# Four split weight tiles, three ahead, and attention's values in an 8 KB room

## The chip, the cores and the metric

The kernel runs on one core of a Trainium2 chip. The metric is the device time of one execution in microseconds (us), lower is better. The core has five engines with a queue each: TensorE (matmul, in the profile PE, its weight loads PEld), VectorE (DVE), ScalarE (ACT), GpSimd (POOL) and SyncE (SP, which here only issues DMAs). They work side by side and wait for one another through semaphores.

## What is computed

A decoder trunk of two layers on x of 512 x 1024 in float32. The reference, cut to what matters:

```python
for l in range(DEPTH):                                   # 2
    x = x + 0.5 * swiglu(rms_norm(x, ffn1_norm[l]), ffn1_wg[l], ffn1_wu[l], ffn1_wd[l])
    h = rms_norm(x, mix_norm[l])
    z = h @ w_in[l]                                      # q | k | v | conv_B | conv_C | conv_h
    attn_out = sliding_window_attention(q, k, v, attn_sink[l])   # window 128, 8 heads of 64, 2 kv heads
    conv_out = short_conv(conv_B, conv_C, conv_h, conv_w[l])     # 3 taps
    x = x + jnp.concatenate([attn_out, conv_out], axis=-1) @ w_out[l]
    x = x + 0.5 * swiglu(rms_norm(x, ffn2_norm[l]), ffn2_wg[l], ffn2_wu[l], ffn2_wd[l])
return rms_norm(x, final_norm)
# swiglu(h, wg, wu, wd) = (silu(h @ wg) * (h @ wu)) @ wd ; d_ff = 2816
```

## The kernel before

**Split operands.** Every product of float32 operands is made of three faster matmuls. A weight tile (`raw`, 4 KB in each of the 128 partitions) is split into a high part `wh`, a cast on ScalarE (line 205), and a low part `wl`, the rest, a subtraction on VectorE (line 206, `split`). The activations are split in the same way. TensorE then adds high x high, high x low and low x high in one bank of PSUM.

**The supply of weights.** `plan` (line 420) writes down ahead of time which raw tiles are loaded (`units`) and in which order tiles are split (`order`). `need_raw` (line 191) issues the loads from SyncE's queue (line 189); a few raw tiles are sums of two weight blocks, and the second block is added by a DMA that GpSimd issues (line 200). There are eight rooms for raw tiles (`stock`, tag "raw"). `need_split` (line 215) splits all tiles up to a given place in the order, loading four units further than the one that it splits. `take_split` (line 280) hands the next split tile to a product and first asks for the splits of the tiles up to `SPLIT_AHEAD` = 2 further. Three rooms each hold `wh` and `wl`, so the split of the tile two ahead waits until TensorE is done with the tile before the present one. A product of one tile is mostly 12 matmuls.

**Order of the work.** The queues are filled from the order in which the program states the work, which is its priority; a compile-time scheduler may put a later instruction first where an earlier one isn't ready. In regions between `by_hand` and `by_itself` TensorE keeps the written order. On the chip each engine takes its queue in the order so fixed.

**The stages.** A feed-forward part is a list of stages (`FIRST`, `INNER`, `LAST`): "p" plain blocks (with `halves`, line 312, three tiles held at once and both halves of the tokens run through them, and then the `up` tile, line 1009), "w" blocks of gate and up in Winograd's form with seven products (`winograd2`, line 1080), "d" the down projection (`down`, `down_end`), "s" the down projection of four blocks in Winograd's form (`share`, line 895, seven chains of two products each; `stream`, line 878). Where `share` gets `after`, it is a *closing group*: it ends a part and feeds the next part's norm. Its chains are `CHAINS_EARLY`; after the fifth chain the norm of the first half of the tokens starts (`Norm.stage`: squares, root, the scaled `xn` of line 624), and in the seventh `pull` transposes them on TensorE (line 648) and splits them (lines 657 and 658, named `hh`, `hl` or `fb`). VectorE adds each chain's banks to the residual stream `x` (line 923; line 1240 for "d"). Three parts are closed so, the first feed-forward part of layer 0 and attention's output projection in both layers; the other parts end with `down_end`.

**Rooms for small tiles.** The tag "g2" has 14 rooms of 2 KB: gates, kept sums, the planes that a Winograd block sends through a transposing DMA (line 1103), the norms' `xn` and gains, attention's turned probabilities. The tag "g8" has four rooms of 8 KB. Attention's values `vv` (line 1407) take a raw tile's room, as do its probabilities. The bias table of attention is made once (`make_bias`, line 863) after the second "d" of the first part: an iota on GpSimd (line 865), then VectorE (line 867 on).

The functions that the diff touches:

Of the kernel before, what the change touches and what calls it, by code (L numbers as in the profile page):

```python
# [9 lines left out]
F32R = mybir.dt.float32r  # L10
# [6 lines left out]
P = 128  # L17
# [3 lines left out]
HD = 64  # L21
NH = 8
NKV = 2
FF = 2816
KC = D // P
NT = S // P
# [21 lines left out]
XT_TAGS = ("sc", "aux", "aux", "mm", "sc", "sc", "aux", "aux")  # L48

OPEN = 3  # L50
SPLIT_AHEAD = 2
LOAD_AHEAD = 4

CHAINS = (
# [19 lines left out]
def trunk_kernel(  # L74
# [28 lines left out]
    wpool = ctx.enter_context(tc.tile_pool(name="wpool", bufs=1))  # L103
# [4 lines left out]
        return ps.tile(shape, F32, tag=tag, bufs={"mm": 4, "sc": 2, "aux": 2}[tag], name=name)  # L108

    def g2(name, dt=F32, shape=(P, S)):  # L110
        return work.tile(list(shape), dt, tag="g2", bufs=14, name=name)

    def g8(name, dt=F32R, shape=(P, 2, 2, S)):
        return work.tile(list(shape), dt, tag="g8", bufs=4, name=name)
# [6 lines left out]
    def stock(name, dt=F32, shape=(P, KC, P)):  # L121
        return wpool.tile(list(shape), dt, tag="raw", bufs=8, name=name)
# [92 lines left out]
    def need_split(g):  # L215
        while state["split"] <= min(g, len(order) - 1):
            n = state["split"]
            u, what = order[n]
            far = what == "far"
            if what in (None, "wide", "room", "far"):  # L220
                need_raw(u if far else u + LOAD_AHEAD)
                raw = raw_of.pop(u)
            elif isinstance(what, tuple):

                what, h, how = what
                far = how == "far"
                last = {"a11": 0, "a12": 4, "s2": 2, "s3": 6, "s1": 2, "a22": 8, "s4": 4}[what]
                need_raw(u + h if far else u + max(last, 4) + h + LOAD_AHEAD)
                a11, s1, a12, s3, a22 = (raw_of.get(u + 2 * i + h) for i in range(5))
                if what == "s2":  # L230
                    late = state["late"] if h else None
                    with tc.issue_after(late) if late else nullcontext():
                        nc.vector.tensor_add(a11, a11, s1)  # L233
                raw = {"a11": a11, "a12": a12, "s2": a11, "s3": s3, "s1": s1, "a22": a22, "s4": a12}[what]
            else:

                need_raw(u + 4 + LOAD_AHEAD)
                a11, a12, s1, s3, a22 = (raw_of.get(u + i) for i in range(5))
                if what == "s2":
                    nc.vector.tensor_add(a11, a11, s1)  # L240
                if what == "s4":
                    nc.vector.tensor_add(a11, a11, a12)
                raw = {"a11": a11, "a12": a12, "s2": a11, "s3": s3, "s1": s1, "a22": a22, "s4": a11}[what]
                if what == FORMS[-1]:
                    for i in range(5):
                        del raw_of[u + i]
            shape = list(raw.shape)
            if what == "room":
                hi, lo = both(f"wx_{n}", shape=(P, 2, 2, S))
            else:  # L250
                hi = wpool.tile(shape, F32R, tag="wh", bufs=3, name=f"wh_{n}")
                lo = wpool.tile(shape, F32R, tag="wl", bufs=3, name=f"wl_{n}")
            if far:
                sent = split_far(hi, lo, raw)
            else:
                state["cast"] = split(hi, lo, raw)
            if isinstance(order[n][1], tuple):
                early = how == "early"
                if what == "s2" if early else what == "s3":
                    if how:  # L260
                        nc.gpsimd.dma_start(out=a12, in_=a11, accum_op=ALU.add)
                    else:
                        nc.vector.tensor_add(a12, a12, a11)
                done = {
                    "s2": (0,) if early else (),
                    "s3": (3,) if early else (0, 3),
                    "s1": (1,),
                    "a22": (4,),
                    "s4": (2,),
                }.get(what, ())  # L270
                for i in done:
                    del raw_of[u + 2 * i + h]
            split_of[n] = (hi, lo)
            state["split"] += 1
            if far:

                with tc.issue_after(sent.ins):
                    need_raw(u + LOAD_AHEAD + (4 + h if isinstance(order[n][1], tuple) else 0))

    def take_split(ahead=SPLIT_AHEAD):  # L280
        n = state["group"]
        state["group"] += 1
        need_split(n + ahead)
        return n, *split_of.pop(n)
# [27 lines left out]
    def halves(norm, n, done):  # L312

        first = state["group"]
        held = [take_split(SPLIT_AHEAD - j)[1:] for j in range(n)]
        accs = [psum("mm", [P, S], f"acc_{first + j}") for j in range(n)]
        for t in range(2):
            for half in range(2):
                for j, (hi, lo) in enumerate(held):
                    for k in range(KC // 2 * half, KC // 2 * (half + 1)):  # L320
                        xh, xl = norm.half(k, t)
                        for i, (w, x_) in enumerate(((hi, xh), (hi, xl), (lo, xh))):
                            nc.tensor.matmul(  # L323
                                accs[j][:, t * H : (t + 1) * H],
                                w[:, k, :],
                                x_,
                                start=t + k + i == 0,
                                stop=k == KC - 1 and i == 2,
                                skip_group_check=True,
                            )  # L330
                    if not t and half and j < 2:
                        norm.pull()
                    if t and half:
                        need_split(first + j + 3)
                        done(j, accs[j])

    def down(acts, blocks, open_):
# [30 lines left out]
    def down_end(acts, blocks, norm, open_):  # L368

        a, b = blocks  # L370
        held = []

        def tile_of(n):
            while len(held) <= n:
                held.append(take_split(max(0, min(SPLIT_AHEAD, 3 - len(held))))[1:])
            return held[n]

        def products(acc, t, n):
# [28 lines left out]
        for o in range(2):  # L407
            accs = {t: bank(t, o) for t in (2, 3)}
            for i in range(2):
                n = 2 * o + i  # L410
                for t in (2, 3):
                    products(accs[t], t, n)
                    if i:
                        yield t, o, accs[t]
                if n in (1, 2):
                    norm.pull()
                if n:
                    need_split(ahead + n - 1)

    def plan():  # L420
        def plain(wg, wu, b):
# [335 lines left out]
    def squares(n):  # L757
# [4 lines left out]
            )  # L762

    first = [
        tuple(wpool.tile([P, KC, P], F32R, tag=f"w{p}", bufs=3, name=f"w{p}_{n}") for p in "hl")
        for n in range(OPEN)
    ]
    opening, begun = [], set()
# [126 lines left out]
    def share(  # L895
# [6 lines left out]
        for step, (acc, operand, start) in enumerate(chains):  # L902
# [7 lines left out]
                tag = {"x": "mm", "y": "sc", "w": "aux", "z": "mm"}[acc]  # L910
                accs[acc] = [psum(tag, [P, S], f"{acc}_{ops.name}_{m}") for m in range(2)]
            for h in range(2):
                _, wh, wl = take_split()
                stream(accs[acc], wh, wl, xh, xl, h, start, after if step == 6 else None)
                each()
                if soon:
                    ops.make(*soon.get((step, h), ()))
                if h == 0 or step in kept:
                    continue
                for o, t, sign in shares[step]:  # L920
                    for m in range(2):
                        part = xt(2 * t + m, o)
                        nc.vector.scalar_tensor_tensor(  # L923
                            part, accs[acc][m], by * sign, part, op0=ALU.mult, op1=ALU.add
                        )
                        if after and (step, (o, t)) in ENDS_EARLY:
                            after(2 * t + m, o)
# [14 lines left out]
    def ffn(norm, stages, whole, after=None, late=None):  # L942
# [137 lines left out]
        def winograd2(b, at, between=None):  # L1080
# [1 line left out]

            name = f"{whole}_{b}"
            accs = {}
            gates = [g2(f"gate_{name}_{t}") for t in range(NT)]
            ups = [None] * NT
            kept = {}
            planes = []
# [23 lines left out]
            for step, (acc, operand, start) in enumerate(CHAINS):  # L1112
# [5 lines left out]
                for h in range(2):  # L1118
                    _, wh, wl = take_split()
                    stream(accs[acc], wh, wl, xh, xl, h, start)  # L1120
                    for u in range(2):
# [3 lines left out]
                        if step == 0:  # L1125
                            keep("p1", u, out)
                        if step == 1:
                            nc.vector.tensor_add(gates[u], out, kept["p1", u])
                            nc.scalar.activation(gates[u], gates[u], AF.Silu)
                        if step == 2:  # L1130
# [6 lines left out]
                        if step == 5:  # L1137
# [2 lines left out]
                            nc.vector.tensor_mul(ups[u], ups[u], gates[u])  # L1140
                            apart(u)
                        if step == 6:
                            nc.scalar.activation(gates[2 + u], out, AF.Silu)
                            nc.vector.tensor_mul(ups[2 + u], ups[2 + u], gates[2 + u])
                            apart(2 + u)
# [230 lines left out]
    def mix(l, norm, after):  # L1376
# [20 lines left out]
        def take_values():  # L1397
# [6 lines left out]
                )  # L1404


            vv = stock(f"vv_{l}", F32R, (P, NT * NKV, 2, HD))
            vsrc = vp.rearrange("p t g d -> p (t g) d")
            nc.scalar.copy(vv[:, :, 0, :], vsrc)
            nc.vector.tensor_sub(vv[:, :, 1, :], vsrc, f32(vv[:, :, 0, :]))  # L1410
# [197 lines left out]
```

## Time and profile before

| what | value |
| --- | --- |
| median of 3 runs | 1654.36 us (1653.59 to 1654.96) |
| the profiled execution, whole | 1655.61 us |
| its span, first to last instruction | 1653.8 us |
| granted clock of TensorE, mean | 0.999 |
| DMA, mean over the span | 184 GB/s |

The profile is of one execution. Its page gives each engine's busy time and share of the span, the chain of work that ended last and the costliest groups; the trace behind it answers for waits (who stood idle until whom), for timelines of an engine, and for tiles. An instruction is named by its line in the kernel, its engine and `out<-in`, by the program's tile names without their numbers.

### The profile page before, as it was taken

The numbers are of one execution on the slowest core, as the hardware profiler recorded it, in microseconds if no ns is written. First come the engines' busy times: TensorE is split into PE (matmuls) and PEld (weight loads), VectorE is DVE, ScalarE is ACT, GpSimd is POOL, SyncE is SP. The second block draws the span as 40 slices with busy tenths as digits, with TensorE's granted clock in tenths as the row PEclk, the third lists the DMA queues.
The fourth block names the chain that finished last, engine by engine and source line by source line (L and its number), as shares of the span: only waits on it lengthen the run. The fifth ranks groups of instructions, "written<-read, shape, count | busy, mean of one in ns | idle before, by whom it ended". The sixth has DMA issues, their size and how long they took to land.

```text
span 1653.8 us, 21619 instructions
## 1 busy us (share of the span) xinstructions
PE 1639.9 (99%) x7912; PEld 1377.6 (83%) x7912; DVE 1307.0 (79%) x1712; ACT 1092.4 (66%) x1527; POOL 192.7 (12%) x172
## 2 busy tenths in 40 slices
PE   9999999999999999999999999999999999999998
PEld 7878888888889888888898888888988888888886
DVE  7977779867799777789797777896587987777895
ACT  6457787556566567776565777864565765777864
POOL 0011111100111101111001111110001101111111
PEclk9999999999999999999999999999999999999999
DMA  9378999821495779999837789996125946899992
GB/s 255 91 189 204 226 214 267 209 78 52 110 241 121 194 187 222 211 227 250 223 85 197 197 211 221 237 248 184 52 65 143 225 115 167 218 225 219 235 261 76
DMA packets 273791, 303.97 MB, mean 184 GB/s; under 512 B 89332, under 2 KB 157972, under 8 KB 273684
## 3 DMA queue, kind: packets, MB, share of 16 engines
q1 hardware_dynamic: 231156, 223.27, 45.8%
q0 software_dynamic: 41824, 78.65, 28.1%
q8 instruction: 62, 1.02, 0.2%
q10 hardware_dynamic: 704, 0.66, 0.1%
q14 instruction: 45, 0.37, 0.1%
HBM read 263.74 MB, written 2.10 MB: 161 GB/s over the span
## 4 chain that ended last, share of the span: by engine, by line
PE 92%; DVE 5%; ACT 1%; issue 1%; DMA 0%; POOL 0%; DVEq 0%; ACTq 0%; POOLq 0%
PE x L884 25%; PE y L884 12%; PE x_s L884 10%; PE w L884 6%; PE y_s L884 5%; PE acc L296 4%; PE acc L297 4%; PE acc L299 4%; PE down L346 3%; PE w_s L884 3%; PE acc L323 3%; PE x_m L884 2%; DVE wl L206 2%; PE up L1009 1%; PE acc L782 1%; DVE x L923 1%
## 5 line engine op out<-in xcount | busy, mean ns | idle before, releaser
L206 DVE TENSOR_TENSOR wl<-raw,wh 128x1024 fp32r<-128x1024 f32 (+1 forms) x493 | 597.4, 1215 | 227.0 <-ACT wh L205 220.6
L205 ACT CAST wh<-raw 128x1024 fp32r<-128x1024 f32 (+1 forms) x493 | 515.1, 1046 | 391.3 <-PE y L884 61.4
L884 PE MATMUL x<-wh,fb 128*128 128x512 f32 x608 | 187.3, 389 | 0.1
L884 PE MATMUL y<-wh,ft 128*128 128x512 f32 x608 | 187.1, 389 | 0.0
L884 PE MATMUL x<-wh,ft 128*128 128x512 f32 x608 | 187.1, 389 | 0.0
L884 PEld LDWEIGHTS y<-wh,ft 128*128 128x128 f32 x608 | 114.1, 188 | 23.7
L884 PEld LDWEIGHTS x<-wh,ft 128*128 128x128 f32 x608 | 114.1, 188 | 23.7
L884 PEld LDWEIGHTS x<-wh,fb 128*128 128x128 f32 x608 | 113.9, 188 | 23.9 <-DVE x L1240 0.5
L884 PE MATMUL x<-wl,fb 128*128 128x512 f32 x304 | 118.3, 389 | 0.0
L884 PE MATMUL x<-wl,ft 128*128 128x512 f32 x304 | 118.3, 389 | 0.0
L884 PE MATMUL y<-wl,ft 128*128 128x512 f32 x304 | 118.3, 389 | 0.0
L1155 ACT COPY raw_a<-pt 128x1024 uint16<-128x1024 uint16 x76 | 103.3, 1359 | 13.0 <-DMA pt<-pl 12.9
L200 POOL DMA_DIRECT2D raw<-in_ffn_wu_dram x39 | 47.2, 1211 | 517.4 <-DMA raw<-in_ffn_wu_dram 360.8
L296 PE MATMUL acc<-hh,wh 128*128 128x512 f32 x240 | 94.6, 394 | 0.0
L299 PE MATMUL acc<-hh,wl 128*128 128x512 f32 x240 | 93.9, 391 | 0.0
L297 PE MATMUL acc<-hl,wh 128*128 128x512 f32 x240 | 93.6, 390 | 0.0
L884 PE MATMUL w<-wh,fb 128*128 128x512 f32 x304 | 93.5, 389 | 0.0
L200 POOL DMA_DIRECT2D raw<-in_ffn_wg_dram x39 | 47.4, 1222 | 275.3 <-DMA raw<-in_ffn_wu_dram 70.7
L884 PE MATMUL x_s<-wh,ft_s 128*128 128x512 f32 x256 | 78.8, 389 | 0.0
L884 PE MATMUL y_s<-wh,ft_s 128*128 128x512 f32 x256 | 78.8, 389 | 0.0
L884 PE MATMUL x_s<-wh,fb_s 128*128 128x512 f32 x240 | 73.9, 389 | 0.0
L233 DVE TENSOR_TENSOR raw<-raw,raw 128x1024 f32<-128x1024 f32 x58 | 70.8, 1221 | 2.3 <-DMA raw<-in_ffn_wd_dram 1.6
(361 smaller groups left out, 3452.3 us busy)
## 6 DMA issues: line engine op xcount, KB each, us to landing
raw<-in_ffn_wu_dram SPq DMA_DIRECT2D x126, 512.0 KB, 4.7
raw<-in_ffn_wd_dram SPq DMA_DIRECT2D x104, 512.0 KB, 6.7
raw<-in_ffn_wg_dram SPq DMA_DIRECT2D x86, 512.0 KB, 4.9
raw<-in_ffn_wu_dram POOLq DMA_DIRECT2D x39, 512.0 KB, 7.3
raw<-in_ffn_wg_dram POOLq DMA_DIRECT2D x39, 512.0 KB, 5.8
raw<-in_w_in_dram SPq DMA_DIRECT2D x36, 512.0 KB, 3.9
raw<-in_ffn_wd_dram POOLq DMA_DIRECT2D x32, 512.0 KB, 8.2
raw<-raw POOLq DMA_DIRECT2D x20, 512.0 KB, 8.2
```

The lines of the kernel that those rows point to most:

```text
L200: nc.gpsimd.dma_start(out=r, in_=rows_of(*more), accum_op=ALU.add)
L205: cast = nc.scalar.copy(hi, raw)
L206: eng.tensor_sub(lo, raw, f32(hi))
L233: nc.vector.tensor_add(a11, a11, s1)
L296: nc.tensor.matmul(acc, hi[:, k, :], rhs[k][0], start=k == first, stop=False)
L297: nc.tensor.matmul(acc, hi[:, k, :], rhs[k][1], start=False, stop=False)
L299: nc.tensor.matmul(acc, lo[:, k, :], rhs[k][0], start=False, stop=k == last)
L323: nc.tensor.matmul(accs[j][:, t * H : (t + 1) * H], w[:, k, :], x_, start=t + k + i == 0, stop=k == KC - 1 and i == 2, skip_group_check=True,)
L346: nc.tensor.matmul(acc, a[:, k, tok], w[:, k, :], start=i + k + n == 0 and fresh[t], stop=i == last and k == 1 and n == 2, skip_group_chec ...
L782: nc.tensor.matmul(opening[n], (lo if part == "w" else hi)[:, k, :], xl if part == "x" else xh, start=n not in begun, stop=k == KC - 1 and ...
L884: nc.tensor.matmul(accs[u], x_[:, 2 * h + k, tok], w[:, k, :], start=start and h + k + i == 0, stop=h + k == 2 and i == 2, skip_group_chec ...
L1155: nc.scalar.copy(room.rearrange("p c (n z) -> p c z n", z=2)[:, :, z, :], turned[0][:, NT * z + 2 * c : NT * z + 2 * c + 2, :],)
```

## The change

The split tiles get a fourth room, and the look-ahead goes from two to three, except in the first eight tiles and, in closing groups, in the steps 4 and 5 (the fifth and sixth chain), where it stays two. The places where tiles are held (`halves`, `down_end`) ask one tile further as well. To make room, the small tiles lose three of their 14 rooms, and `winograd2` makes its four gates when they are first written and not all at the start. Attention's values move from the tag "raw" to the tag "g8".

```diff
-SPLIT_AHEAD = 2
+SPLIT_AHEAD = 3
...
     def g2(name, dt=F32, shape=(P, S)):
-        return work.tile(list(shape), dt, tag="g2", bufs=14, name=name)
+        return work.tile(list(shape), dt, tag="g2", bufs=11, name=name)
...
-                hi = wpool.tile(shape, F32R, tag="wh", bufs=3, name=f"wh_{n}")
-                lo = wpool.tile(shape, F32R, tag="wl", bufs=3, name=f"wl_{n}")
+                hi = wpool.tile(shape, F32R, tag="wh", bufs=4, name=f"wh_{n}")
+                lo = wpool.tile(shape, F32R, tag="wl", bufs=4, name=f"wl_{n}")
...
     def take_split(ahead=SPLIT_AHEAD):
         n = state["group"]
+        ahead = min(ahead, 2) if n < 8 else ahead
...
                     if t and half:
-                        need_split(first + j + 3)
+                        need_split(first + j + SPLIT_AHEAD + 1)
...
-                held.append(take_split(max(0, min(SPLIT_AHEAD, 3 - len(held))))[1:])
+                held.append(take_split(min(SPLIT_AHEAD, 4 - len(held)))[1:])
...
                 if n:
-                    need_split(ahead + n - 1)
+                    need_split(ahead + n)
...
-        tuple(wpool.tile([P, KC, P], F32R, tag=f"w{p}", bufs=3, name=f"w{p}_{n}") for p in "hl")
+        tuple(wpool.tile([P, KC, P], F32R, tag=f"w{p}", bufs=4, name=f"w{p}_{n}") for p in "hl")
...
-                _, wh, wl = take_split()
+                _, wh, wl = take_split(SPLIT_AHEAD - 1 if after and step in (4, 5) else SPLIT_AHEAD)
...
-            gates = [g2(f"gate_{name}_{t}") for t in range(NT)]
+            gates = [None] * NT
...
                         if step == 1:
+                            gates[u] = g2(f"gate_{name}_{u}")
...
                         if step == 6:
+                            gates[2 + u] = g2(f"gate_{name}_{2 + u}")
...
-            vv = stock(f"vv_{l}", F32R, (P, NT * NKV, 2, HD))
+            vv = g8(f"vv_{l}", F32R, (P, NT * NKV, 2, HD))
```

## The prediction

> **What bounds the kernel now.** I read the page first, then the waits of TensorE, then the timelines of the engines around those waits.
>
> ```profile
> span 1653.8 us, 21619 instructions
> PE 1639.9 (99%) x7912; PEld 1377.6 (83%) x7912; DVE 1307.0 (79%) x1712; ACT 1092.4 (66%) x1527; POOL 192.7 (12%) x172
> ```
>
> TensorE is idle for 13.9 us of the span, the start and the end of the program included, so no deeper buffer can win more than a fraction of a per cent. The waits of TensorE (tile and line; what it waited for; us in total, times, longest) name the candidates:
>
> ```profile
> PE acc L323 <- DVE wl L206: 1.9, 3, 0.6
> PE x_m L884 <- DVE wl L206: 1.6, 2, 0.8
> PE idle L141 <- DVE warm L728: 1.2, 1, 1.2
> PE down L346 <- DVE x L1240: 0.9, 2, 0.5
> PE up L1009 <- DVE wl L206: 0.8, 3, 0.3
> PE xt L747 <- DMA x<-in_x_dram: 0.3, 1, 0.3
> ```
>
> Three of the six are for `wl`, the low part of a split weight tile, which is what a fourth tile can reach. The view counts idle time only after the modelled end of a matmul; what a wait costs is read from start to start in TensorE's timeline (start, us, then the instruction, the idle time before it in brackets):
>
> ```profile
> 479.27 0.39 PE L884 MATMUL y_m<-wl,ft_m 128*128 128x512 f32 x1
> 479.50 1.07 PE L884 MATMUL x_m<-wh,ft_m 128*128 128x512 f32 x4
> 481.34 0.50 PE L884 MATMUL x_m<-wl,ft_m 128*128 128x512 f32 x1 [0.78 <-DVE wl L206]
> 481.68 0.63 PE L884 MATMUL x_m<-wh,ft_m 128*128 128x512 f32 x2
> ...
> 504.15 0.40 PE L323 MATMUL acc<-fb,wh 128*128 128x256 f32 x2
> ...
> 505.58 0.40 PE L323 MATMUL acc<-fb,wh 128*128 128x256 f32 x2
> 506.08 0.39 PE L323 MATMUL acc<-fb,wl 128*128 128x256 f32 x1
> ...
> 507.38 0.40 PE L323 MATMUL acc<-fb,wh 128*128 128x256 f32 x2
> 508.42 0.39 PE L323 MATMUL acc<-fb,wl 128*128 128x256 f32 x1 [0.63 <-DVE wl L206]
> ...
> 511.16 1.03 PE L648 MATMUL xt<-ident,xn 128*128 128x128 f32 x8
> ...
> 524.40 0.40 PE L1009 MATMUL up<-fb,wh 128*128 128x256 f32 x2
> 525.08 0.38 PE L1009 MATMUL up<-fb,wl 128*128 128x256 f32 x1 [0.28 <-DVE wl L206]
> ```
>
> Wide matmuls start 0.23 us apart (479.27 to 479.50), so a product of 12 takes 2.7 us. In `x_m` four run ahead of the first `wl`, which was due at 479.50 + 4 x 0.23 = 480.41 and came at 481.34: 0.93 lost, and 0.11 more at the next start (0.34 instead of 0.23). Matmuls of 256 columns start 0.12 apart (two in 0.40 of which one lasts 0.28). The `wl` of `acc` was due at 505.82 and 507.62 and came 0.26 and 0.80 late, that of `up` 0.44 late; with 0.1 for each restart these are 1.26 and 0.54.
>
> The waits view gives the repeats. `x_m` occurs twice, 2 x 1.04 = 2.1 us. `up` occurs three times, 3 x 0.54 = 1.6 us. The pair in `acc` occurs three times (the view counts the longer of each pair), 3 x 1.25 = 3.7 us. Together that is 7.4 us that TensorE loses for split weights. The `down` waits are for something else, below.
>
> **The change part by part.** The fourth pair of `wh` and `wl` with three ahead moves every split one product earlier against TensorE; it adds no instruction. Each split is still one cast on ScalarE and one subtraction on VectorE, and each still waits for the room of the product just finished. What goes is the case in which an engine stood idle for a room and was then too busy:
>
> ```profile
> 463.15 1.06 ACT L205 CAST wh<-raw 128x1024 fp32r<-128x1024 f32 x1 [4.57 <-PE acc L297]
> ...
> 511.79 1.08 ACT L657 CAST fb<-xt 128x512 fp32r<-128x512 f32 x2 [3.03 <-PE xt L648]
> ...
> 521.60 1.05 ACT L205 CAST wh<-raw 128x1024 fp32r<-128x1024 f32 x1 [0.28 <-PE acc L323]
> ```
>
> ```profile
> 463.45 0.69 DVE L1556 TENSOR_TENSOR m<-acc,cc 128x512 f32<-128x512 f32 x1 [2.53 <-PE acc L299]
> ...
> 478.34 1.22 DVE L687 TENSOR_TENSOR sums_m<-sums_m,m 128x1024 f32<-128x1024 f32 x1
> ...
> 480.07 1.22 DVE L206 TENSOR_TENSOR wl<-raw,wh 128x1024 fp32r<-128x1024 f32 x1
> ...
> 498.89 2.48 DVE L923 SCALAR_TENSOR_TENSOR x<-x_m,x 128x512 f32<-128x512 f32 x4
> 501.29 1.22 DVE L206 TENSOR_TENSOR wl<-raw,wh 128x1024 fp32r<-128x1024 f32 x1
> 502.42 2.48 DVE L658 TENSOR_TENSOR fb<-xt,fb 128x512 fp32r<-128x512 f32 x4
> 504.81 1.22 DVE L206 TENSOR_TENSOR wl<-raw,wh 128x1024 fp32r<-128x1024 f32 x1
> 505.94 1.29 DVE L923 SCALAR_TENSOR_TENSOR x<-z_m,x 128x512 f32<-128x512 f32 x2
> 507.14 1.22 DVE L206 TENSOR_TENSOR wl<-raw,wh 128x1024 fp32r<-128x1024 f32 x1
> 508.27 0.16 DVE L616 TENSOR_TENSOR v<-ss 128x2 f32<-128x2 f32 x1
> ...
> 509.45 2.74 DVE L624 SCALAR_TENSOR_TENSOR xn<-x,y,gain 128x512 f32<-128x512 f32 x4
> ```
>
> (1) `x_m`, at the fourth product of attention's closing group. Ahead of that group ScalarE stands 4.57 us and VectorE 2.53; a cast and a subtraction fit in there. VectorE then works from 463.45 without a pause up to the late `wl` at 480.07, so one subtraction less (1.13 from start to start, 501.29 to 502.42) brings it forward by 1.13, and in the program it now also stands ahead of the sum at 478.34. Lost were 1.04: I take the whole 2.1 us. If VectorE's order eats it, 0.
>
> (2) `up`, the fourth tile after three that are held together. With three rooms its cast can't start before the first held tile is done (521.60). With four it can start when the three begin, and ScalarE is idle for 3.03 us before 511.79. I take the whole 1.6 us.
>
> (3) `acc`, the first tiles after a closing group. In that group's fifth and sixth product the look-ahead stays at two, so nothing is gained there; at the seventh two splits are asked for at once. VectorE has no pause between 498.89 and 508.27, so a `wl` done earlier pushes something else back. Either the splits of the fifth and sixth product are pulled forward into short pauses, the fourth room allowing it, and all 3.7 us go; or the second `wl` runs in front of the four residuals `fb` of 502.42. Then the first two of those end at 503.55 + 2 x 0.60 = 504.75 instead of 503.62, while TensorE wants them at 504.27: 0.5 late and 0.1 for the restart; the `x` of 505.94 starts 1.13 later, and so does the `xn` of 509.45, whose second of four then ends at 509.45 + 1.13 + 2 x 0.67 = 511.9. Its four transposes, 0.11 apart, end at 512.4; today the eight of 511.16 are through at 512.0. So the two late `wl` go, and TensorE is still some 0.5 later than today: 3 x 0.5 = 1.5 us worse. Between -3.7 and +1.5 I take -1.9, half of the gain: the `wl` of 507.14 belongs to a later statement than the norm's `v` of 508.27 and still runs first, so idle moments are filled, but few are left.
>
> (4) `down`:
>
> ```profile
> 110.19 1.21 POOL L200 DMA_DIRECT2D raw<-in_ffn_wg_dram  x1 [10.99 <-DMA raw<-in_ffn_wu_dram]
> ...
> 111.80 0.46 DVE L867 CAST dist<-dist_i 128x256 f32<-128x256 int32 x1 [3.47 <-POOL dist_i L865]
> ...
> 112.13 0.39 PE L346 MATMUL down<-wl,a 128*128 128x512 f32 x1
> 112.90 0.73 PE L346 MATMUL down<-wh,a 128*128 128x512 f32 x2 [0.38 <-DVE x L1240]
> ```
>
> VectorE stands 3.47 us behind the bias table's iota, and GpSimd's iota behind a DMA issue that waits for a landing; the reads `x` of the banks queue after it. This start was due at 112.36 and came 0.54 late, 0.65 with its restart; of the two waits and one shorter one behind them I make 1.8. An earlier load could win that, a later one lose as much; 0.
>
> (5) Eleven small rooms instead of fourteen, and gates made when first written. A grouped product writes fourteen of them, the last four being planes that leave by a transposing DMA, placed one to four products into the next block (this row is from the answer on the tile `pl`):
>
> ```profile
> DMA to landing us min/median/max: 3.2/4.4/8.5
> ```
>
> Room by room in turn, the sixth write of a block then takes the room of the first plane: gone by 2.7 + 8.5 = 11.2 us, asked for after six products, 16.3 us. 5 us are to spare; 0. If that fails, an evacuation of a bank comes late.
>
> (6) Attention's values in an 8 KB room: the same cast and subtraction. Four such rooms exist, and attention holds two (its mixed outputs) until the closing group's sums take one. One more raw tile may load ahead there, where no row shows TensorE waiting. 0. In the first eight tiles the look-ahead stays at two: 0.
>
> Sum: 2.1 + 1.6 + 1.9 = 5.6 us. The profiled execution took 1655.61 (its span and 1.8 around it), 1.25 above the median, so 1650.0 on its own clock and **1654.36 - 5.6 = 1648.8** on the median's.
>
> A rule of the Trainium skill speaks against part (3): "TensorE: Matmul & The Clock Gate", Architectural detail, says that VectorE and ScalarE run strictly first in, first out. By that rule nothing jumps a queue on the chip, and only the order fixed before the run counts, which no row of this trace shows for the new kernel; with it (3) is +1.5, the first rival's time.
>
> **The rivals.** *The closing groups only trade waits* (3 at its bad end): -2.1 - 1.6 + 1.5 = -2.2, 1652.2. For it: VectorE is full there. Against: the filled gap above.
>
> *All split waits go, and `down` with them*: -7.4 - 1.8 = -9.2, 1645.2. Against: (3).
>
> *Slower: the raw tiles aren't there yet.* ScalarE's waits have this row:
>
> ```profile
> ACT wh L205 <- DVE raw L233: 15.8, 7, 2.9
> ```
>
> Seven casts already stand behind a sum of two raw tiles. Asked for 2.7 us earlier, with loads that don't come earlier, each blocks ScalarE for up to 2.9 + 2.7 = 5.6 us, and VectorE's `wl` and the bank reads `x` behind it. TensorE returns to a bank after two products (5.4 us), of which two reads take 1.3, so from a block of 4.1 us on it waits: 1.5 each, 10.5 for seven, less 5.6 won: +4.9, 1659.3. Against: a load waits for a raw room that a split frees, and splits come earlier as well; today none of these seven reaches TensorE.
>
> *It doesn't do what it says*: the engines' order leaves the splits where they are; 1654.4.
>
> **How the numbers follow.** Forecast 0.47; all waits gone 0.13; trading 0.17; no effect 0.05; slower 0.18. About 0.2% (3.3 us) is what a measurement of this kernel can tell from no change. Faster is 0.47 + 0.13 = 0.60; within is 0.17 + 0.05 = 0.22; slower 0.18. The range goes from all gone (1644.9, with 0.3 of scatter) to 1656.0, a slower case of which a third of the blocks bite; most of the 0.18 stays outside.
>
> **What would show it.** Right: no row of TensorE waiting for `wl` under `x_m` and `up`; the ScalarE pause before attention's closing group holds a cast; the rows under `acc` shorter but there. Wrong: new rows of TensorE waiting for `fb`, `hl` or `xn` (trading), for `x` (slower), ScalarE's waits for `raw` sums well above 15.8, or waits on `pl`.

## The result, and the profile after

The changed kernel takes 1652.12 us (median of 13 executions, 1650.4 to 1654.99), the kernel before beside it 1655.96 (13 executions, 1653.59 to 1657.79). The ratio is 0.9977, interval 0.9968 to 0.9985: 3.8 us faster, hardly more than the 0.2% that can be told from no change. A second measurement gave 1652.93 against 1655.69, ratio 0.9983 (0.9974 to 0.9991). The forecast was 1648.8: the sign was right, the time is 3.3 us above it and inside the range.

The profiled execution of the changed kernel took 1650.43, against 1655.61 before: 5.2 less, where the sum said 5.6. From its page, span and busy time:

```profile
span 1648.7 us, 21650 instructions
PE 1637.2 (99%) x7912; PEld 1376.7 (84%) x7912; DVE 1303.5 (79%) x1712; ACT 1089.3 (66%) x1527; POOL 193.0 (12%) x172
```

And all that is left of TensorE's waits (tile, line, what it waited for; us in total, times, longest):

```profile
PE xt L649 <- DVE xn L625: 2.1, 3, 0.8
PE idle L141 <- DVE warm L729: 1.2, 1, 1.2
PE xt L748 <- DMA x<-in_x_dram: 1.0, 1, 1.0
```

No wait for `wl` is left, under `x_m`, `up` or `acc`; `down` is gone too; the norm's `xn` is new. Read from start to start in TensorE's timeline, as the prediction did, the three kinds of `wl` wait gave back their whole 2.1 + 1.6 + 3.7 us, small `wl` waits too short for the list another 0.3, and `down` 1.8. Lost again were 3.4 before the `xn` transposes (0.8, 1.3 and 1.3), 0.6 more in attention's two closing groups and 0.3 near 29 us. Net 5.2; the spans differ by 5.1. The longer wait for `x` at the start costs nothing: the transposes ahead of it begin 0.64 earlier, and the first product starts at 6.66 instead of 6.65.

**Where `xn` became late.** VectorE, then ScalarE, then TensorE of the changed kernel, at the end of the closing group of attention in layer 0:

```profile
491.74 0.15 DVE L617 TENSOR_TENSOR v<-ss 128x2 f32<-128x2 f32 x1
492.65 1.22 DVE L206 TENSOR_TENSOR wl<-raw,wh 128x1024 fp32r<-128x1024 f32 x1 [0.76 <-ACT wh L205]
...
493.94 0.68 DVE L924 SCALAR_TENSOR_TENSOR x<-x_m,x 128x512 f32<-128x512 f32 x1
...
495.87 2.73 DVE L625 SCALAR_TENSOR_TENSOR xn<-x,y,gain 128x512 f32<-128x512 f32 x4
```

```profile
491.57 1.05 ACT L205 CAST wh<-raw 128x1024 fp32r<-128x1024 f32 x1
492.52 0.29 ACT L618 ACTIVATE r<-v,eps 128x2 f32<-128x2 f32 x1
```

```profile
495.45 0.39 PE L885 MATMUL z_m<-wl,fb_m 128*128 128x512 f32 x1
496.67 1.32 PE L649 MATMUL xt<-ident,xn 128*128 128x128 f32 x8 [0.84 <-DVE xn L625]
```

VectorE of the kernel before, at the same place:

```profile
493.92 0.16 DVE L616 TENSOR_TENSOR v<-ss 128x2 f32<-128x2 f32 x1 [0.15 <-ACT sq L592]
...
495.10 2.74 DVE L624 SCALAR_TENSOR_TENSOR xn<-x,y,gain 128x512 f32<-128x512 f32 x4
```

Before, `xn` began 1.18 after `v` (493.92 to 495.10); now it takes 4.13 (491.74 to 495.87). A cast of a later weight tile stands ahead of the norm's root `r` on ScalarE, and its subtraction and three reads `x` of banks stand ahead of `xn` on VectorE. The order fixed before the run had a free room for that split and took it. TensorE starts 1.22 after its last matmul instead of 0.23.

**Why `down` is no longer late.** VectorE of the changed kernel, at the end of the first "d":

```profile
108.41 2.48 DVE L1243 SCALAR_TENSOR_TENSOR x<-down,x 128x512 f32<-128x512 f32 x4
111.08 1.23 DVE L206 TENSOR_TENSOR wl<-raw,wh 128x1024 fp32r<-128x1024 f32 x1 [0.20 <-ACT wh L205]
112.22 0.68 DVE L1243 SCALAR_TENSOR_TENSOR x<-down,x 128x512 f32<-128x512 f32 x1
112.82 0.28 DVE L868 CAST dist<-dist_i 128x256 f32<-128x256 int32 x1
```

Five of the bank reads `x` now stand ahead of `dist`, and `dist` finds the iota done. Before, only two did; VectorE stood 3.47 us behind the iota, and the other reads queued behind it. The iota itself was no earlier than before (GpSimd began it at 111.24, before at 110.93).

### The profile page after: what moved, and what is told of

The parts are those of the page before. It is cut to its first block, busy times and chain, and to the rows that moved or that the text cites. A ratio compares the mean times of both kernels' runs of the same rounds, so it can differ in the third digit from the quotient of the medians.

```text
span 1648.7 us, 21650 instructions
## 1 busy us (share of the span) xinstructions
PE 1637.2 (99%) x7912; PEld 1376.7 (84%) x7912; DVE 1303.5 (79%) x1712; ACT 1089.3 (66%) x1527; POOL 193.0 (12%) x172
## 4 chain that ended last, share of the span: by engine, by line
PE 96%; DVE 2%; ACT 1%; DMA 1%; issue 0%; SPq 0%; ACTq 0%; DVEq 0%
PE x L885 25%; PE y L885 13%; PE x_s L885 10%; PE w L885 6%; PE y_s L885 5%; PE acc L324 5%; PE acc L297 4%; PE acc L298 4%; PE acc L300 4%; PE down L347 3%; PE w_s L885 3%; PE up L1010 1%; PE xt L649 1%; PE y_m L885 1%; PE x_m L885 1%; PE acc L783 1%
```

## Experiments

My theory at this point: the fourth room does the work, and what the change lost again it lost in the order of the closing groups. Rivals: the earlier asking does the work (e2); the moves of small tiles and of attention's values do part of it (e3, e12); the losses come from DMA landings (e7, e10).

**e1: four rooms, look-ahead two as before.** From the changed kernel:

```diff
-SPLIT_AHEAD = 3
+SPLIT_AHEAD = 2
...
-        ahead = min(ahead, 2) if n < 8 else ahead
...
-                held.append(take_split(min(SPLIT_AHEAD, 4 - len(held)))[1:])
+                held.append(take_split(max(0, min(SPLIT_AHEAD, 3 - len(held))))[1:])
...
-                    need_split(ahead + n)
+                    need_split(ahead + n - 1)
...
-                _, wh, wl = take_split(SPLIT_AHEAD - 1 if after and step in (4, 5) else SPLIT_AHEAD)
+                _, wh, wl = take_split()
```

> Fourth room, eleven small rooms and the values' move as in the changed kernel, but every look-ahead as before (two). Theory 1, the room alone is enough, because the order fixed before the run fills idle moments with later splits as soon as their room is free: TensorE's waits for wl under x_m and up go, 3 to 4 us less than before (ratio 0.9975 to 0.998). Rival, the asking is what counts: all wl waits of before are still there (4.3 us in the waits view) and the time is that of before (ratio 0.9995 to 1.0005).

Measured: 1650.51 (1649.83 to 1651.94), ratio to the kernel before 0.9966 (0.9954 to 0.9979). Waits of its TensorE:

```profile
PE xt L648 <- DVE xn L624: 1.7, 2, 0.8
PE idle L141 <- DVE warm L728: 1.2, 1, 1.2
PE xt L747 <- DMA x<-in_x_dram: 0.7, 1, 0.7
```

No wait for `wl`, though no split is asked for earlier than before. The room does it, with the moves that make place for it and without the earlier asking: the compile-time order fills it by itself.

**e2: look-ahead three, three rooms.** The changed kernel with three rooms (the list of the first tiles likewise):

```diff
-                hi = wpool.tile(shape, F32R, tag="wh", bufs=4, name=f"wh_{n}")
-                lo = wpool.tile(shape, F32R, tag="wl", bufs=4, name=f"wl_{n}")
+                hi = wpool.tile(shape, F32R, tag="wh", bufs=3, name=f"wh_{n}")
+                lo = wpool.tile(shape, F32R, tag="wl", bufs=3, name=f"wl_{n}")
```

> The changed kernel with three rooms for wh and wl instead of four; the look-ahead stays three. Theory 1 (the room is what was missing): the casts wait for their room as before, the wl waits come back (4.3 us in the waits view), the time is before's or up to 3 us above (ratio 0.9995 to 1.002). Rival (asking earlier in the program is enough): the wl waits stay away and the ratio is 0.997 to 0.998.

Measured: 1658.13 (1656.63 to 1661.18), ratio 1.0012 (1.0004 to 1.0021). Its TensorE:

```profile
PE xt L649 <- DVE xn L625: 1.3, 3, 0.4
PE x_s L885 <- DVE wl L206: 1.3, 3, 0.5
...
PE acc L324 <- DVE fb L659: 1.0, 2, 0.5
PE y_m L885 <- ACT wh L205: 0.8, 2, 0.4
```

Asking earlier does take away the waits under `x_m`, both of them, and two of three under `up`. But `xn`, `x_s`, `fb` and others wait in their place: asking alone loses. Ahead of `fb`, VectorE now takes two subtractions in a row (from 501.61), and `acc` waits 0.5 for it.

**e3: the moves alone.** The kernel before with eleven small rooms, gates made when first written and the values in the 8 KB room:

```diff
-        return work.tile(list(shape), dt, tag="g2", bufs=14, name=name)
+        return work.tile(list(shape), dt, tag="g2", bufs=11, name=name)
...
-            gates = [g2(f"gate_{name}_{t}") for t in range(NT)]
+            gates = [None] * NT
...
-            vv = stock(f"vv_{l}", F32R, (P, NT * NKV, 2, HD))
+            vv = g8(f"vv_{l}", F32R, (P, NT * NKV, 2, HD))
```

> The kernel before with eleven small rooms, late gates and the values in an 8 KB room, and no change to the splits. Theory: the moves cost and win nothing, the waits of TensorE stay as before, ratio 0.9995 to 1.0005. Rival: the two waits of down at 113 and 115 us, which the changed kernel lost, went because the small rooms changed the order around the bias table; then they are gone here as well and the ratio is about 0.999.

Measured: 1655.86 (11 executions), ratio 0.9997 (0.9988 to 1.0006): nothing.

```profile
PE acc L323 <- DVE wl L206: 1.9, 3, 0.6
PE x_m L884 <- DVE wl L206: 1.6, 2, 0.8
PE w_s L884 <- DVE wl L206: 1.4, 1, 1.4
```

The waits for `wl` are all there. The `down` waits happened to be missing with VectorE's order unchanged: the iota came at 109.78 instead of 110.93, since the DMA that GpSimd waited for (10.99 us before) had landed sooner. So `down` also hangs on a landing that differs between executions.

**e4: three ahead in the closing groups' fifth and sixth product too.**

```diff
-                _, wh, wl = take_split(SPLIT_AHEAD - 1 if after and step in (4, 5) else SPLIT_AHEAD)
+                _, wh, wl = take_split()
```

> The changed kernel with a look-ahead of three in the fifth and sixth chain of closing groups too. Theory (VectorE's order decides in a closing group): more splits stand ahead of the norm's xn, the transposes wait longer for xn than the 2.1 us of the changed kernel, and it is 1 to 4 us slower than the changed kernel (ratio to before 0.998 to 1.000). Rival (the splits are pulled forward into free rooms whatever is asked): same xn waits and same time as the changed kernel, ratio 0.9972 to 0.9982.

Measured: 1651.58 (1650.29 to 1652.35), ratio 0.997 (0.9959 to 0.9982), `xn` waits 2.1 us in three places as in the changed kernel. The exception changes nothing that can be measured: the split that it meant to hold back is pulled forward anyway.

**e6: the bias table behind the last bank read**, in the kernel before:

```diff
-                nc.vector.scalar_tensor_tensor(
+                read = nc.vector.scalar_tensor_tensor(
                     xt(t, o), acc, 0.5, xt(t, o), op0=ALU.mult, op1=ALU.add
...
             if b == (1,) and late:
-                late()
+                with tc.issue_after(read.ins):
+                    late()
```

> The kernel before, with the bias table's instructions on VectorE held behind the last bank read of the second down projection. Theory (the two waits of down are an order effect: dist stands in front of bank reads and waits for GpSimd's iota, which waits for a landing): the down waits of 113 and 115 us go, the other waits stay, 0.5 to 1.8 us less than before (ratio 0.9989 to 0.9997). Rival (late banks have another cause there, such as the split's place): the down waits stay.

Measured: 1654.07 against 1655.37, ratio 0.9992 (0.9983 to 1.0001). The rows of TensorE waiting for `down` are gone, those for `wl` stay. But the iota also came earlier here, at 109.01, as it did in e3, so this profile can't tell the order from the landing. The changed kernel's can: there the iota is late and no read waits. That the order is worth time is within the scatter.

**e7: the seventh chain's splits held behind the norm**, in the changed kernel (`self.last` is the last instruction that writes `xn`):

```diff
-                _, wh, wl = take_split(SPLIT_AHEAD - 1 if after and step in (4, 5) else SPLIT_AHEAD)
+                with tc.issue_after(after.last.ins) if after and step == 6 else nullcontext():
+                    _, wh, wl = take_split(SPLIT_AHEAD - 1 if after and step in (4, 5) else SPLIT_AHEAD)
```

> The changed kernel with the splits that the seventh chain of a closing group asks for held behind the norm's xn on VectorE. Theory (the new waits for xn at 497 and 1311 us come from a split and bank reads that the order fixed before the run puts between the norm's root and its xn): those two go, 2 x 1.17 us, and the time is 1 to 2.5 us below the changed kernel's (ratio to before 0.996 to 0.997). Rival (VectorE simply has too much work ahead of the transposes): the waits stay or turn into waits for fb or wl, ratio 0.9972 to 0.9982.

Measured: 1652.42 (1650.65 to 1655.42), ratio 0.9981 (0.9973 to 0.999): no better than the changed kernel. From start to start, the waits at 497 and 1311 us went (1.3 each), but 0.6 for `fb` and 0.8 for `xn` came in their place, up to about 511 and 1326: a trade. The third wait for `xn`, in the first closing group, stayed. And its profile caught something else. VectorE, ScalarE and TensorE of e7:

```profile
227.58 1.23 DVE L240 TENSOR_TENSOR raw<-raw,raw 128x1024 f32<-128x1024 f32 x1 [2.64 <-DMA raw<-in_ffn_wu_dram]
```

```profile
229.44 1.14 ACT L1099 COPY pl<-u 128x512 uint16<-128x512 uint16 x2 [3.64 <-DVE u L1143]
```

```profile
238.70 0.50 PE L1052 MATMUL x<-ft,wh 128*128 128x256 f32 x2 [2.58 <-ACT p L1036]
```

VectorE stood 2.64 us in front of a sum of raw tiles whose load hadn't landed; the reads `u` queued behind it, then ScalarE's planes, then the kept `p`, and TensorE lost 2.58. In the changed kernel's first profile the same sum, in the same order, started at 224.30 without a wait, and ScalarE's planes had waited less:

```profile
226.15 1.14 ACT L1098 COPY pl<-u 128x512 uint16<-128x512 uint16 x2 [0.91 <-DVE u L1142]
```

That is the mechanism of the slower rival (a raw tile that isn't there yet, with VectorE's queue behind it), and by the Trainium skill too ("TensorE: Matmul & The Clock Gate", Architectural detail: VectorE and ScalarE take their queues strictly first in, first out) nothing could pass; these rows agree: 2.64 us of a DMA's delay came out as 2.73 more on ScalarE (3.64 against 0.91) and as 2.58 on TensorE.

**e8: four rooms, look-ahead two, and the hold of e7**: e1 with this one edit (and `self.last` as there).

```diff
-                _, wh, wl = take_split()
+                with tc.issue_after(after.last.ins) if after and step == 6 else nullcontext():
+                    _, wh, wl = take_split()
```

> The kernel with the fourth room and a look-ahead of two everywhere, and the splits of the seventh chain held behind xn. Theory: no wait for wl, x or xn over 0.2 us is left after the start; ratio 0.995 to 0.9965, the fastest so far. Rival: as for the run with the look-ahead of three.

Measured: 1649.19 (1649.04 to 1650.01), ratio 0.9963 (0.9951 to 0.9976). Its TensorE:

```profile
PE xt L747 <- DMA x<-in_x_dram: 1.3, 1, 1.3
PE acc L323 <- DVE wl L206: 1.3, 2, 0.6
PE idle L141 <- DVE warm L728: 1.2, 1, 1.2
PE x_s L884 <- DVE wl L206: 0.2, 1, 0.2
```

No `xn` is late; of the `acc` waits two of three came back, at 0.9 us each from start to start instead of the pair of 1.25. So the hold trades waits here too, and from e1 (0.9966) this can't be told apart. But e7, on the same chip, differs from e8 in the look-ahead alone: its fastest execution (1650.65) is above the slowest of e8 (1650.01), and the medians are 3.2 us apart. With the hold, asking one tile earlier costs time.

**e9: four rooms for `wh`, three for `wl`**, look-ahead two, from e1 (the list of the first tiles likewise, here and in e13).

```diff
-                lo = wpool.tile(shape, F32R, tag="wl", bufs=4, name=f"wl_{n}")
+                lo = wpool.tile(shape, F32R, tag="wl", bufs=3, name=f"wl_{n}")
```

> Look-ahead two, four rooms for wh but three for wl. Theory (the chain of cast and subtraction behind a room is what is late): the cast no longer waits, but the subtraction still waits for its room, so the wl waits become about 1 us shorter each and mostly go; ratio 0.997 to 0.9985. Rival (both rooms are needed): the wl waits of before stay, ratio 0.999 to 1.001.

Measured: 1666.92 (1663.12 to 1668.13), ratio 1.0068 (1.0055 to 1.008). Neither theory had this. VectorE, ScalarE and TensorE of e9, at one of its three worst places:

```profile
776.79 1.23 DVE L233 TENSOR_TENSOR raw<-raw,raw 128x1024 f32<-128x1024 f32 x1 [2.76 <-DMA raw<-in_ffn_wd_dram]
```

```profile
778.13 1.04 ACT L205 CAST wh<-raw 128x1024 fp32r<-128x1024 f32 x1 [3.70 <-DVE raw L233]
```

```profile
779.80 0.50 PE L884 MATMUL w_s<-wl,fb_s 128*128 128x512 f32 x1 [2.69 <-DVE wl L206]
```

The order now puts the sum of two raw tiles ahead of a subtraction that TensorE needs, the sum waits 2.76 us for a load, and all behind it is late by that. Three such places cost TensorE 8.5 us of waits.

**e13: three rooms for `wh`, four for `wl`**, the other half of the table, from e1.

```diff
-                hi = wpool.tile(shape, F32R, tag="wh", bufs=4, name=f"wh_{n}")
+                hi = wpool.tile(shape, F32R, tag="wh", bufs=3, name=f"wh_{n}")
```

> Four rooms for the low parts alone, three for the high parts, look-ahead two. Theory: the late part was always the low one, but its subtraction reads the high part and so can't run before the cast, which waits for its room: the waits of TensorE for wl stay as in the kernel before, the time is that of the kernel before with its moves, 1655 to 1656.5. Rival: the subtraction's own wait for a room was what cost; then wl waits go and the time falls to 1651.

Measured: 1655.95, ratio 1.0002 (0.9994 to 1.0011), and the old waits:

```profile
PE acc L323 <- DVE wl L206: 1.9, 3, 0.6
PE x_m L884 <- DVE wl L206: 1.9, 2, 1.1
...
PE up L1009 <- DVE wl L206: 0.8, 3, 0.3
```

The late tile was always the low one, yet a room for it alone is worth nothing: its subtraction reads the high part, whose cast waits for the other room. TensorE, VectorE and ScalarE keep the order of the kernel before, instruction for instruction. So in this program both rooms have to be there for a gain.

**e12: attention's values back in a raw tile's room**, all else as in the changed kernel.

```diff
-            vv = g8(f"vv_{l}", F32R, (P, NT * NKV, 2, HD))
+            vv = stock(f"vv_{l}", F32R, (P, NT * NKV, 2, HD))
```

> The changed kernel with attention's values back in a raw tile's room. Theory: a raw tile less can load ahead during attention, no wait of TensorE hangs on it: within 1 us of the changed kernel beside it, whose order of instructions it shares on all engines but GpSimd. Rival: the room bought loads that come in time; then ScalarE's and VectorE's waits for raw tiles after attention (about 480 and 1295 us) grow and the time is 2 us or more above the changed kernel.

Measured: 1656.07 (1655.2 to 1659.89), ratio 1.0005 (0.9996 to 1.0013), where the changed kernel beside it on the same chip has 0.9983 (0.9974 to 0.9991). The rival is right and my theory is not: without this move the change is worth nothing. Its TensorE waits, besides the `xn`, for attention's closing group:

```profile
PE y_m L885 <- DVE ft_m L206: 1.2, 2, 0.8
...
PE y_m L885 <- DVE x L924: 0.8, 2, 0.4
PE x_m L885 <- DVE wl L206: 0.4, 2, 0.2
PE y_m L885 <- ACT ft_m L205: 0.3, 1, 0.3
```

TensorE, VectorE and ScalarE take the same instructions in the same order in both kernels; what differs is GpSimd, which issues the second block of a summed raw tile. Layer 1, GpSimd and ScalarE of e12:

```profile
1278.04 1.20 POOL L200 DMA_DIRECT2D raw<-in_w_out_dram  x1 [0.52 <-DMA raw<-in_w_out_dram]
```

```profile
1287.70 1.05 ACT L205 CAST wh<-raw 128x1024 fp32r<-128x1024 f32 x1 [4.36 <-DMA raw<-in_w_out_dram]
1288.65 1.04 ACT L205 CAST ft_m<-sums_m 128x1024 fp32r<-128x1024 f32 x1
```

And the same places in the changed kernel:

```profile
1269.74 1.20 POOL L200 DMA_DIRECT2D raw<-in_w_out_dram  x1 [0.23 <-PE acc L298]
```

```profile
1281.45 1.06 ACT L205 CAST wh<-raw 128x1024 fp32r<-128x1024 f32 x1 [0.56 <-ACT wh L205]
1282.41 1.05 ACT L205 CAST ft_m<-sums_m 128x1024 fp32r<-128x1024 f32 x1
```

With a room less for raw tiles the last load of attention's output projection is issued 8.3 us later (1278.04 against 1269.74). Its cast, one tile earlier now, stands in front of a DMA for 4.36 us, and the cast of `ft_m` behind it, which TensorE needs, waits with it. Layer 0 shows the same: issue at 463.11 against 455.39, cast at 470.25 against 466.84. (The view names TensorE's `w_m` there, but the load landed at 470.16, just ahead of the cast.) From start to start TensorE loses 1.8 us in attention's closing group of layer 0 and 2.5 in that of layer 1, 4.3 of the 5.0 us between the two profiled executions. So what the change loses there is the later load.

**e10 and e11: the changed kernel and e8 once more, side by side**, nothing altered.

> The changed kernel a second time, nothing altered. Theory: what is left of its loss sits in the order of the closing groups and stands in any execution (xn about 497 and 1311 us, near 1.2 us each), while the split casts of the sums of raw tiles hang on a DMA landing that differs between executions: VectorE's sum at line 240 near 225 us waits between 0 and 2.7 us, and TensorE pays near 237 us whatever is over about 0.5. The time then lies between 1650 and 1655 with a median of 1651.5 to 1652.5. Rival: the spread between executions is of the chip and shows in any kernel; then the kernel with four rooms, look-ahead two and the held splits, beside it, spreads as widely as this one.

> Four rooms, look-ahead two, the splits of the seventh chain held behind the norm, a second time and beside the changed kernel. Theory: its median lies 2 to 3 us under that of the changed kernel (1649 to 1650 against 1652), because xn is on time and splits ask for raw sums no earlier than in the old kernel; spread below 2 us. Rival: the first five executions were lucky; then it lies within 1 us of the changed kernel and spreads over 4 us.

Measured: 1652.93 (12 executions, 1650.65 to 1657.43), ratio 0.9983 (0.9974 to 0.9991), and 1649.5 (5 executions, 1648.69 to 1650.26), ratio 0.9962 (0.9949 to 0.9974). TensorE of the changed kernel, then of e11:

```profile
PE xt L649 <- DVE xn L625: 2.1, 3, 0.8
PE idle L141 <- DVE warm L729: 1.2, 1, 1.2
```

```profile
PE acc L323 <- DVE wl L206: 1.2, 2, 0.6
PE idle L141 <- DVE warm L728: 1.2, 1, 1.2
PE x_s L884 <- DVE wl L206: 1.0, 1, 1.0
```

The three `xn` waits are those of the first profile to the tenth of a microsecond: they belong to the order. The changed kernel spreads over 6.8 us in 12 executions and e8 over 1.6 in 5 on the same chip, so the spread isn't the chip's alone; nor is it new with the change, since the kernel before spreads over 4.8 in 29. The version with four rooms, look-ahead two and the hold is 3.4 us under the changed kernel beside it (1649.5 against 1652.93), and its slowest execution (1650.26) is below the fastest there. The landing at line 240, though, cost nothing in this profile either; that it makes the longer executions is not shown.

## Why the prediction came out as it did

- **(1) `x_m`, (2) `up`: right.** All 2.1 and 1.6 us went. Of the signs named, one reads otherwise than I wrote: the pause of 4.57 us ahead of attention's closing group is still there, now ahead of the 131st cast instead of the 130th, since that cast waits for the room of the tile one further on. All splits run one tile ahead, and `x_m`'s subtraction starts at 472.54 instead of 480.07.
- **(3) `acc`: the step that was mis-sized.** Taken at -1.9, it came to -3.7 + 3.4 = -0.3. The trade of waits that the first rival named is there, and in e1 too, at two of the three places; but it goes through `xn` and ScalarE's root, not through `fb`, whose delay I had worked out. (The path through `fb`, 0.5 late, is that of e2, with three rooms.) I had looked for the displaced instruction in the row behind the late `wl`; it was further ahead, in the chain v, r, xn, where ScalarE and VectorE hand to each other and a cast of 1.05 fits between. Nor did the look-ahead of two in the fifth and sixth product keep anything back: dropping that exception changes nothing that can be measured (e4).
- **(4) `down`: taken at nothing, -1.8 in the profile.** That was luck. In the changed kernel it is the order: bank reads now ahead of `dist`, with an iota as late as before. In e3 a landing did it without any change of order, so the kernel before doesn't lose the 1.8 in every execution.
- **(5) eleven small rooms: right.** e3 with them is at 0.9997, and no row of TensorE shows a plane `pl`.
- **(6) the values' room: the step that failed.** Costed at nothing because no row of the old kernel shows TensorE waiting there. But the change itself moved the casts earlier and so needed the load earlier: with the values in the old place e12 loses all the gain, 3.1 us between the two medians. Alone (e3, with (5)) it is worth nothing. It is what lets (1) cost nothing. The forecast didn't suffer, since the change brings the move along, but that was luck: I had not asked what is lost without it.
- **The slower rival** had the right mechanism, two places of it seen: without the room in e12 (blocks of 4.36 us in layer 1), and at line 240 in e7. One of its signs came: ScalarE's waits for the sums at line 233 rose from 15.8 us to 17.5 in the first profile and 22.1 in e10, the longest from 2.9 to 5.2 and 5.4. I had let a block of 4.1 reach TensorE; in these two profiles none did. For the changed kernel it was wrong as a whole; (6) is part of the reason.
- **The time.** The result lies 3.3 us above the forecast. Of these, 1.6 lie in the base: it was a median of three executions, 1654.36, where thirteen give 1655.96. The other 1.8 are gain that didn't come, 3.8 between the medians where the sum said 5.6. The profiled executions differ by 5.2, but the changed kernel's is the second shortest of thirteen (1650.43, median 1652.12). And that 5.2 is near 5.6 is luck, by errors of opposite sign: (3) fell short by 1.6 and 0.9 was lost where the sum has no term (attention's closing groups, 29 us), while (4) and small `wl` waits won 2.1 that it doesn't have either. What the longer executions spend is in no profile but perhaps that of e7 (1654.07, of which 2.58 at one landing); so this stays open. Also not tried: four rooms and look-ahead two with the values in the old place.
- **The range.** Its upper end, 1656.0, is a third of the slower rival's net 4.9 above the kernel before. A third of the blocks, as I wrote, would be 3.5 less 5.6, or 1652.3.

## What to carry to other kernels

A deeper buffer is a set: here the room for both parts and, with the look-ahead of three, the supply that feeds it one step earlier. What lacked one of these was worth nothing (e3, e12, e13) or lost (e2, e9). Asking earlier in the program wasn't part of the set: e1 gained without it, and with the splits held it cost 3 us (e7 against e8). When an edit makes work run earlier, follow each of its inputs back to the DMA issue, on whichever queue issues it, before pricing any edit on the way at nothing. And where a scheduler fixes the order, a free room is filled whether asked for or not: look which short hand-over between two engines the pulled instruction lands in. Holding it back there removed the wait but brought others; that the hold by itself gains time is not shown (e7, e8).

## What the runs showed of the hardware

A DMA that lands late was passed on nearly whole by the engines' queues, through three engines and 11 us: in e7, 2.64 us on VectorE, 2.73 more than in the changed kernel on ScalarE, and 2.58 on TensorE. And how long one and the same DMA takes differs between executions. The same sum, in the same order on all engines up to there, waited 2.64 us in e7, 0.50 in e4 and nothing in both profiles of the changed kernel. In these two profiles of one kernel, the load that GpSimd issued at 1368.65 took 9.0 us to land in the first, and 5.5 in the second (issued at 1368.04).
